# Pool branch's window means as band products, output weights' casts behind the query and key copies, and 20 taps off VectorE, in a two-block transformer kernel

## The chip, the cores and the metric

The kernel runs on one core of a Trainium2 chip. The metric is the device time of one launch in microseconds, from a batch of timed runs; beside it stands one execution taken by the hardware profiler, whose rows are quoted below. In the rows PE is TensorE's matmul, PEld its weight load, DVE is VectorE, ACT ScalarE, POOL GpSimd and SP SyncE, whose queue issues all DMA transfers here. Times in rows are in us from the start of the span unless marked ns.

## The reference

Two different transformer blocks run one after the other on 256 tokens of width 1024, in float32. The first has a stick-breaking attention and a latent attention side by side, a gated feed-forward with a short convolution, and a gate by a second input. The second block, in which the change lies, is:

```
h   = rmsnorm(x) * (1 + scale) + shift                    # scale, shift from c @ mod_w
z   = h @ w_in                                            # split into the inputs of three branches
y_conv = silu(layernorm(conv31(a_val * sigmoid(a_gate)))) # depthwise, 31 taps, 256 channels
y_att  = attention over the 64 keys that an index score picks, 8 heads
y_pool = per group g of 64 channels, window w = 2, 4, 8, 16:
         mean of the last min(t + 1, w) tokens of u, minus u, then @ pool_w[g]; times pool_scale
x  += g1 * (concat(y_conv, y_att, y_pool) @ w_out)
x  += g2 * moe(rmsnorm(x) ...)                            # 32 experts, 2 of them per token
out = rmsnorm(x)
```

The pool branch takes 256 channels of `z`, four groups with one window each.

## The kernel before

Matrix products of the two blocks are made to float32's precision from two parts: a weight or an activation is split into a rounded part (a ScalarE cast) and the rest (a VectorE subtraction, both in `split`), and `mm3` adds three products. Tokens lie in two blocks of 128. A tensor that is contracted over channels lies transposed, channels on partitions, as `hZ` does for the second block's input; projections whose result is wanted with channels on partitions go through `ch_unit` (weights stationary, 256 tokens moving), those with tokens on partitions through `tok_unit` (a token block stationary, up to 256 weight columns moving).

Only TensorE's instructions stand in an order written by hand. For the second block's mixing part that order is the string `ORDER`: each word calls one step. `up` is the pool branch's projection, `qk0` to `qk3` the queries and keys of two heads each, `va` the values, `d0 d1` the scores of the two token blocks, `sm0 sm1` their softmax, `po` the pool branch's last product, `dT` and `do` the transposes and the product with the values, `w0` to `w3` the output weights' load and split, `c60` and so on the product of chunk 6 of the mixed channels for token block 0 with its output weights, `tp` the convolution's taps, `ct co` its transposes and what follows them, and `ea eh el e1 to e4 es` take a buffer into the ring of expert weights and issue its load. The other engines' instructions, SyncE's loads among them, are put in order by the framework's planner, which works with costs of its own and the program's order; each engine then runs its list in order.

What the change touches:

- `up_proj` (L1317): 48 products into one PSUM bank, one copy `pu` to SBUF, channels on partitions and tokens along the row behind 16 zeros. On GpSimd follow sums of shifted copies (`s_a`, `s_b`: windows 2, 4, 8 and 16 by doubling, each on the partitions that need it), a product with 1 / min(t + 1, w) for the first 16 tokens (`rcp`, made at the kernel's start with `winv`), one with 1 / w for the others, and the subtraction of `pu`.
- `pool_out` (L1344): eight products with `pool_w`; ScalarE and VectorE then write chunks 6 and 7 of `mix2`, the two-part input of the output projection.
- `conv_taps` (L1290): the convolution as 31 taps on two channel halves. Half 0 runs wholly on VectorE. Of half 1 the last `N_TAP` taps are ScalarE multiplies into one of six buffers `pr`, which GpSimd adds up in `cb`:

```
act(pr, src[:, 1], AF.Copy, scale=tap[1])
G.tensor_tensor(cb, cb, pr, op=ALU.add)
```

- `qk2` (L1367): three products into one bank, then two ScalarE copies into `q2` and `k2T`; the scores read these.
- `out_weights` (L1400): loads two chunks of output weights into one of three raw buffers and splits them. These buffers are given one after the other to expert weights as well.
- `w2k2` (L1199): tiles of 2 x 256 + 32 columns in five buffers, used by the index scores' relus (`ixr`, eight tiles), `sg`, `pu`, `s_a`, `s_b` and later ones.

The expert stage streams 192 pieces of 1 MB through a ring of 23 buffers, which come free one by one as the mixing part ends: an `es` tile after `dT1`, raw buffers after their splits, the two `mix2` tiles when the last product of the output projection has read them.

Of the kernel before, what the change touches and what calls it, by code (L numbers as in the profile page):

```python
# [10 lines left out]
F32 = mybir.dt.float32  # L11
# [4 lines left out]
ALU = mybir.AluOpType  # L16
# [19 lines left out]
N_A = 5  # L36
N_B = 3
N_C = 3
N_TAP = 12
NORM_ACT = {'d0': 1, 'd1': 1}  # L40
N_POOL = 0
N_2K = 5
# [4 lines left out]
MOE_K = 2  # L47
X_AT = {(2, 9): 4, (31, 9): 1, (31, 10): 1}
LAST = 'y01 y12 x2 m02 y24 m24'
ORDER = 'qi0 kT0 qi1 kT1 ix0 ix1 cv0 li0 li1 cv1 ea ea lo0 lo1 ae lw ea ea ea va0 up eh el qk0 qk1 qk2 qk3 va1 d0 sm0 d1 po sm1 w3 e1 e2 c60 c61 w1 dT0 do0 c70 c71 c20 w2 dT1 c30 do1 tp e3 e4 e4 rl g1 c21 c31 c40 w0 ct e1 e1 c50 c51 c41 es es co'  # L50
W_AT = (2,)
MIX_ENG = 'VV VV'
SET_LATE = (0, 0)
# [14 lines left out]
def block_pair_kernel(ctx, tc, A, out, dbg=None):  # L68
# [63 lines left out]
    def bank(name):  # L132
        return psp.tile([P, 512], F32, tag="b", name=name)
# [58 lines left out]


    PW = 16
    winv = cp.tile([P, 2], F32, name="winv")
    for i, wdt in enumerate((2, 4, 8, 16)):
        G.memset(winv[64 * (i % 2):64 * (i % 2) + 64, i // 2:i // 2 + 1], 1.0 / wdt)
    rcp = cp.tile([P, 2, PW], F32, name="rcp")
    G.iota(rcp[:, 0, :], pattern=[[1, PW]], base=1, channel_multiplier=0, allow_small_or_imprecise_dtypes=True)
    V.reciprocal(rcp[:, 0, :], rcp[:, 0, :])  # L200
    V.tensor_scalar(rcp[:, 1, :], rcp[:, 0, :], winv[:, 1:2], None, op0=ALU.max)
    V.tensor_scalar(rcp[:, 0, :], rcp[:, 0, :], winv[:, 0:1], None, op0=ALU.max)
# [996 lines left out]
    def w2k2(name):  # L1199
        return wk.tile([P, 2 * SEQ + 32], F32, tag="w2kb", name=name, bufs=N_2K)  # L1200
# [108 lines left out]
        G.tensor_tensor(ca[:, 1, :], ca[:, 1, :], cb, op=ALU.add)  # L1309


    TS = slice(PW, PW + SEQ)
    pw = wk.tile([P, 2, 64], F32, name="pw")
    load(pw, A["pool_w"])
    pooled = []

    def up_proj():  # L1317
        upb = bank("pup")
        raw = raw_pk("w_in2_c", 4, (2, KC, P), "r_up")
        for j in range(2):  # L1320
            ch_unit(raw[:, j], upb[:, j * SEQ:(j + 1) * SEQ], hZ, f"w_up2{j}")
        pu, s_a, s_b = [w2k2(nm).rearrange("p (c t) -> p c t", c=2) for nm in ("pu", "s_a", "s_b")]
        for t_ in (pu, s_a, s_b):
            G.memset(t_[:, :, 0:PW], 0.0)
        S.copy(pu[:, :, PW:], upb.rearrange("p (c t) -> p c t", c=2))

        def sh(t, c, rs, k):
            return t[rs, c, PW - k:PW + SEQ - k]

        full, top = slice(0, P), slice(64, P)  # L1330
        G.tensor_tensor(s_a[:, :, TS], pu[:, :, TS], pu[:, :, PW - 1:PW + SEQ - 1], op=ALU.add)
        G.tensor_tensor(s_b[:, 1, TS], sh(s_a, 1, full, 0), sh(s_a, 1, full, 2), op=ALU.add)
        G.tensor_tensor(s_b[top, 0, TS], sh(s_a, 0, top, 0), sh(s_a, 0, top, 2), op=ALU.add)
        G.tensor_copy(s_a[top, 0, TS], s_b[top, 0, TS])
        G.tensor_tensor(s_a[:, 1, TS], sh(s_b, 1, full, 0), sh(s_b, 1, full, 4), op=ALU.add)
        G.tensor_tensor(s_b[top, 1, TS], sh(s_a, 1, top, 0), sh(s_a, 1, top, 8), op=ALU.add)
        G.tensor_copy(s_a[top, 1, TS], s_b[top, 1, TS])
        G.tensor_tensor(s_a[:, :, PW:2 * PW], s_a[:, :, PW:2 * PW], rcp, op=ALU.mult)
        for c in range(2):
            G.tensor_scalar(s_a[:, c, 2 * PW:], s_a[:, c, 2 * PW:], winv[:, c:c + 1], None, op0=ALU.mult)  # L1340
        G.tensor_tensor(s_a[:, :, TS], s_a[:, :, TS], pu[:, :, TS], op=ALU.subtract)
        pooled.append(s_a)

    def pool_out():  # L1344
        pb = [bank(f"ppl{i}") for i in range(2)]
        for c in range(2):
            for par in range(2):
                rs = slice(64 * par, 64 * par + 64)
                T.matmul(pb[par][rs, c * SEQ:(c + 1) * SEQ], pw[rs, c, :], pooled[0][rs, c, TS], start=(c == 0),
                         stop=True, skip_group_check=True)  # L1350
        for c in range(2):
            for par in range(2):
                rs = slice(64 * par, 64 * par + 64)
                src, g_ = pb[par][rs, c * SEQ:(c + 1) * SEQ], cv("pool_scale_2", c, rs)
                hi, lo = [t[rs, 6 + c, :] for t in mix2]
                act(hi, src, AF.Copy, scale=g_)
                V.scalar_tensor_tensor(lo, src, g_, hi.bitcast(F32), op0=ALU.mult, op1=ALU.subtract)
# [5 lines left out]
    def lat_load():  # L1363
        wu = raw_pk("w_lat2", 0, (4, 512), "r_wu")
        lw.extend(wu[:, 2 * i:2 * i + 2] for i in range(2))

    def qk2(c):  # L1367
        o = bank(f"pq2{c}")
        for k in range(2):
            T.matmul(o[:, :SEQ], lw[0][:, k, c * P:(c + 1) * P], lnT[:, k, :], start=(k == 0), stop=(k == 1))  # L1370
        T.matmul(o[:, SEQ:], lw[1][:, 0, c * P:(c + 1) * P], lnT[:, 2, :], start=True, stop=True)
        S.copy(q2[0][:, c, :], o[:, :SEQ])
        S.copy(k2T[:, c, :], o[:, SEQ:])

    def val2(b):
        o = bank(f"pv2{b}")
# [23 lines left out]
    def out_weights(u):  # L1400
        raw = raw_rows("w_out_2", u, f"r_out{u}")
        for j in range(2):
            wpo[2 * u + j] = split(raw[:, j, :], f"w_out{2 * u + j}", (D,), eng=G if 2 * u + j in OUT_G else V)

    def out_chunk(c, b):
        if not acc:
# [42 lines left out]
    def router_load():  # L1449
# [3 lines left out]
        load(M2["rb"], rows_of(A["router_b"], 36))  # L1453

    M2 = {}
    steps = {"lw": lat_load, "up": up_proj, "po": pool_out, "tp": conv_taps, "ct": conv_T,
             "co": conv_out, "rl": router_load, "ea": lambda: grow(ewa, 1),
             "eh": lambda: grow(ap_, 1, "ah", (P, KC, SEQ)), "el": lambda: grow(ap_, 1, "al", (P, KC, SEQ)),
             "ae": lambda: act_set("exp_and_others", SET_LATE[1]),
# [387 lines left out]
def lay_out(inputs):  # L1847
# [35 lines left out]
    o["fcols"] = cw.reshape(4, 44, P).transpose(2, 0, 1)  # L1883
    o["mod_w"] = I["mod_w_2"][0].reshape(KC, P, 3, 2048).transpose(2, 0, 1, 3).reshape(3 * KC, P, 2048)
    w = I["w_in_2"][0]
    o["w_in2_c"] = ch(w, *((a, a + P) for a in (0, 256, 896, 1152, 1480)))
    o["w_in2_q"] = tok(w, [(512, 256)])
    o["w_in2_k"] = tok(w, [(768, 128), (1408, 72)])
    o["pool_w"] = I["pool_w_2"][0].reshape(2, P, 64).transpose(1, 0, 2)
# [31 lines left out]
```

## Time and profile before

| | us |
|---|---|
| median of 3 runs (lowest to highest) | 942.63 (941.95 to 943.38) |
| profiled execution | 942.79 |
| its span, first to last instruction | 941.1 |

| engine | busy us | share of the span |
|---|---|---|
| TensorE matmul | 785.0 | 83% |
| TensorE weight load | 570.9 | 61% |
| VectorE | 466.7 | 50% |
| ScalarE | 321.8 | 34% |
| GpSimd | 110.1 | 12% |

The span falls into the first block (to some 366 us), the second block's mixing part (to some 490 us) and the experts. The shares are averages over these stages. A timeline row gives start, duration, engine, line, operation, output and inputs, a form, and in brackets how long the engine had been idle and what ended that; rows of one line that follow each other are merged, with their count. Many rows of ScalarE have line 80, a helper's, and are told apart by their tiles.

### The profile page before, as it was taken

To read this page: it belongs to the slowest core of one execution; us is meant where nothing else is said; L and a number is where in the kernel's file an instruction comes from. 1 tells how busy PE (TensorE), PEld (TensorE's weight loads), DVE (VectorE), ACT (ScalarE), POOL (GpSimd) and SP (SyncE) were. 2 spreads that over 40 slices of the span, in tenths; PEclk is the share of its full clock that TensorE was granted. 3 is DMA by queue.
4 is the path that set the end of the run, shared out by engine and by line. 5 is a ranking of instruction groups with operands and counts; after the bars stand their busy time and mean duration, and the time that the engine had idled before them with its cause. 6 is when DMAs were issued, how large, how long until landed. Compare 5 with 4: busy or idle time off the path is not lost. (4 is left out here: it accounts for less than half of the span.)

```text
span 941.1 us, 17238 instructions
## 1 busy us (share of the span) xinstructions
PE 785.0 (83%) x7172; PEld 570.9 (61%) x7172; DVE 466.7 (50%) x1011; ACT 321.8 (34%) x636; POOL 110.1 (12%) x176
## 2 busy tenths in 40 slices
PE   6999989999999998996988988677766767766864
PEld 6898859999999775894675645243333433433422
DVE  5777476678888788589963323112121121211113
ACT  5649645555555575465741101000010000100100
POOL 1321320222112112207010000000000000000000
PEclk9999999999999998997999999879799897988887
DMA  8862388588676755745389999999999999999994
GB/s 309 283 206 85 122 333 318 194 338 313 254 276 231 268 203 194 301 168 179 129 332 422 422 420 425 419 425 421 423 422 422 425 422 422 423 421 426 420 423 166
DMA packets 45894, 301.22 MB, mean 320 GB/s; under 512 B 5360, under 2 KB 6388, under 8 KB 11124
## 3 DMA queue, kind: packets, MB, share of 16 engines
q1 hardware_dynamic: 45812, 300.08, 79.9%
q8 instruction: 58, 0.95, 0.4%
q14 instruction: 24, 0.20, 0.1%
HBM read 299.01 MB, written 1.05 MB: 319 GB/s over the span
## 5 line engine op out<-in xcount | busy, mean ns | idle before, releaser
L1710 PE MATMUL eu<-ew,XT 128*32 128x256 f32 x2048 | 141.8, 409 | 51.6 <-DMA ew<-in_exp_dram 51.5
L1710 PEld LDWEIGHTS eu<-ew,XT 128*32 128x32 f32 x2048 | 60.9, 115 | 123.9 <-DMA ew<-in_exp_dram 57.0
L80 ACT ACTIVATE hm<-eu 128x128 f32<-128x128 f32 x32 | 8.9, 278 | 334.2 <-PE eu L1710 334.2
L1737 PE MATMUL ey<-ew,hmT 128*32 128x256 f32 (+2 forms) x1088 | 80.7, 432 | 37.1 <-DMA ew<-in_exp_dram 25.2
L1723 DVE TENSOR_TENSOR hm<-hm,eu 128x128 f32<-128x128 f32 x32 | 9.2, 288 | 145.4 <-ACT hm L80 145.4
L1737 PEld LDWEIGHTS ey<-ew,hmT 128*32 128x32 f32 x1088 | 33.1, 121 | 71.6 <-DMA ew<-in_exp_dram 34.8
L1748 DVE TENSOR_TENSOR eys<-ey,g2y 128x256 f32<-128x256 f32 x31 | 13.2, 425 | 107.5 <-PE ey L1737 107.5
L1008 POOL TENSOR_TENSOR ac<-cv_g,cv_v 128x256 f32<-128x256 f32 x22 | 36.0, 1637 | 154.3 <-ACT w_g_w L80 108.3
L222 POOL TENSOR_SCALAR ep_fin<-msf 128x2 f32<-128x2 f32 x1 | 0.2, 238 | 446.2 <-DVE msf L1827 446.2
L275 PE MATMUL u<-hF_h,w_g_w 128*128 128x256 f32 x168 | 47.6, 283 | 0.0
L273 PE MATMUL u<-hF_h,w_g_w 128*128 128x256 f32 x168 | 47.5, 283 | 0.0
L274 PE MATMUL u<-hF_l,w_g_w 128*128 128x256 f32 x168 | 47.5, 283 | 0.0
L274 PE MATMUL u<-hF_l,w_v_w 128*128 128x256 f32 x160 | 45.3, 283 | 0.0
L275 PE MATMUL u<-hF_h,w_v_w 128*128 128x256 f32 x160 | 45.3, 283 | 0.0
L273 PE MATMUL u<-hF_h,w_v_w 128*128 128x256 f32 x160 | 45.2, 283 | 0.0
L1639 PE MATMUL moe<-eys,gT 32*128 32x256 f32 (+1 forms) x528 | 43.4, 444 | 1.4 <-DVE eys L1761 1.4
L1720 DVE COPY gT<-pgs 128x256 f32<-128x256 f32 x32 | 13.6, 425 | 52.4 <-PE pgs L1706 52.3
L80 ACT ACTIVATE XT<-px,c_SH,c_G 128x128 f32<-128x128 f32 x32 | 14.7, 458 | 63.9 <-DVE XT L1681 63.9
L1673 PEld LDWEIGHTS px<-hr,x 128*128 128x128 f32 x256 | 33.0, 212 | 4.3 <-issue 3.3
L1673 PE MATMUL px<-hr,x 128*128 128x128 f32 x256 | 34.7, 299 | 0.7 <-DVE hr L1665 0.7
L274 PE MATMUL dn<-w_dn_w,ach 128*128 128x512 f32 x88 | 34.6, 393 | 0.0
L1639 PEld LDWEIGHTS moe<-eys,gT 32*128 32x128 f32 x528 | 28.8, 216 | 9.5 <-issue 7.0
(566 smaller groups left out, 1978.1 us busy)
## 6 DMA issues: line engine op xcount, KB each, us to landing
ew<-in_exp_dram SPq DMA_DIRECT2D x189, 1024.0 KB, 19.7
r_mod<-in_mod_w_dram SPq DMA_DIRECT2D x24, 1024.0 KB, 8.7
r_gv<-in_w_up_dram SPq DMA_DIRECT2D x22, 1024.0 KB, 6.3
r_d<-in_w_down_dram SPq DMA_DIRECT2D x11, 1024.0 KB, 5.0
r_wo<-in_w_o_dram SPq DMA_DIRECT2D x4, 1024.0 KB, 4.8
r_pg<-in_w_ple_gate_dram SPq DMA_DIRECT2D x4, 1024.0 KB, 6.1
r_out<-in_w_out_dram SPq DMA_DIRECT2D x4, 1024.0 KB, 4.8
r_v<-in_w_in_t_dram SPq DMA_DIRECT2D x2, 1024.0 KB, 7.2
```

Source lines behind the costliest of these rows:

```text
L80: i = getattr(nc.scalar, name)(*a, **kw)
L273: T.matmul(o, l[0], r[0], start=start, stop=False, skip_group_check=True)
L274: T.matmul(o, l[0], r[1], start=False, stop=False, skip_group_check=True)
L275: T.matmul(o, l[1], r[0], start=False, stop=stop, skip_group_check=True)
L1008: G.tensor_tensor(a_, gt, vl, op=ALU.mult)
L1639: T.matmul(moe[c][:, b * 256:b * 256 + 256][:, js], gT[rs, TB[b]], yt[rs, js], start=(start and b == 0), stop=stop, skip_group_check=True)
L1673: T.matmul(pt[:, j * P:(j + 1) * P], x[b][:, k * P:(k + 1) * P], hr[:, b], start=(b == 0), stop=(b == 1))
L1710: T.matmul(u[32 * g_:32 * g_ + 32, 0:2 * P], XT[:, k, 32 * i:32 * i + 32], etiles[6 * e + k // 2][k % 2][:, :, P * g_:P * g_ + P], start=( ...
L1720: V.tensor_copy(gT, pg[:, :SEQ])
L1723: V.tensor_mul(hm, hm, u[:, P:2 * P])
L1737: T.matmul(y[32 * c:32 * c + 32, 0:64 * (js.stop - js.start)], hmT[:, 32 * k:32 * k + 32], w2e[k].rearrange("p j (c i) -> p c j i", c=4)[: ...
L1748: V.tensor_mul(yt, y[:, 0:256], g2y)
```

## The change

The pool branch's projection now gives tokens on partitions (`puT`), from weights laid out for that (`w_in2_u`). The windows' means minus the input are a product over tokens with a matrix that is 1 / w on a band, less the identity: `band` for all tokens beyond the first 16, `edge` with the shorter counts for these. Both are built in the second block by selects on GpSimd. A new step `pb` makes the 12 products between `qk1` and `qk2`, and `po` moves from behind `d1` to behind `sm0`. `puT` and `pooled` are taken from the `w2kb` buffers before the first step. The casts of output weights get an order edge behind the last query and key copy. `N_TAP` goes from 12 to 20.

```diff
-N_TAP = 12
+N_TAP = 20
-ORDER = '... up eh el qk0 qk1 qk2 qk3 va1 d0 sm0 d1 po sm1 w3 e1 e2 c60 c61 ...'
+ORDER = '... up eh el qk0 qk1 pb qk2 qk3 va1 d0 sm0 po d1 sm1 w3 e1 e2 c60 c61 ...'
-    (winv and rcp at the kernel's start: four memsets, an iota, three VectorE operations)
+    WIN = (2, 4, 8, 16)
+    band, edge = wk.tile([P, 4, P + 16], F32, name="band"), wk.tile([P, 4, 16], F32, name="edge")
+    rt = wk.tile([P, 16], F32, name="rt")
+    G.iota(rt, pattern=[[1, 16]], base=1, channel_multiplier=0, allow_small_or_imprecise_dtypes=True)
+    V.reciprocal(rt, rt)
+    for i, wdt in enumerate(WIN):
+        G.memset(band[:, i], 1.0 / wdt)
+        V.tensor_scalar(edge[:, i], rt, 1.0 / wdt, None, op0=ALU.max)
+    for t_, n in ((band, P + 16), (edge, 16)):
+        G.affine_select(t_, t_, pattern=[[0, 4], [1, n]], compare_op=ALU.is_ge, fill=0.0, base=0, channel_multiplier=-1)
+        for i, wdt in enumerate(WIN):
+            if wdt < n:
+                G.affine_select(t_[:, i], t_[:, i], pattern=[[-1, n]], compare_op=ALU.is_ge, fill=0.0, base=wdt - 1,
+                                channel_multiplier=1)
+        m = min(n, P)
+        V.tensor_sub(t_[:, :, :m], t_[:, :, :m], ident[:, None, :m].to_broadcast([P, 4, m]))
+    puT, pooled = [w2k2(nm)[:, :2 * SEQ].rearrange("p (c t) -> p c t", c=2) for nm in ("puT", "pooled")]
 
     def up_proj():
-        upb = bank("pup")
-        raw = raw_pk("w_in2_c", 4, (2, KC, P), "r_up")
-        for j in range(2):
-            ch_unit(raw[:, j], upb[:, j * SEQ:(j + 1) * SEQ], hZ, f"w_up2{j}")
-        (pu, s_a, s_b: three memsets, the copy pu, eleven GpSimd operations)
+        raw = raw_pk("w_in2_u", 0, (KC, 256), "r_up")
+        o = [bank(f"pup{b}") for b in range(NB)]
+        tok_unit(raw, 256, [t[:, :256] for t in o], hZ, "w_up2")
+        for b in range(NB):
+            S.copy(puT[:, b], o[b][:, :256])
+
+    def pool_band():
+        pb = bank("pband")
         for c in range(2):
+            o = pb[:, c * SEQ:(c + 1) * SEQ]
+            for b, cs_, t_, j in ((0, slice(0, 16), edge, 0), (0, slice(16, P + 16), band, 16), (1, slice(P, SEQ), band, 0)):
+                for par in range(2):
+                    rs = slice(64 * par, 64 * par + 64)
+                    T.matmul(o[rs, cs_], puT[:, b, 128 * c + 64 * par:][:, :64],
+                             t_[:, 2 * c + par, j:j + cs_.stop - cs_.start], start=(c == b == 0 and t_ is edge),
+                             stop=True, skip_group_check=True)
+        S.copy(pooled, pb.rearrange("p (c t) -> p c t", c=2))
@@ qk2
-        S.copy(q2[0][:, c, :], o[:, :SEQ])
-        S.copy(k2T[:, c, :], o[:, SEQ:])
+        qk_ins[:] = [S.copy(q2[0][:, c, :], o[:, :SEQ]), S.copy(k2T[:, c, :], o[:, SEQ:])]
@@ out_weights
-            wpo[2 * u + j] = split(raw[:, j, :], f"w_out{2 * u + j}", (D,), eng=G if 2 * u + j in OUT_G else V)
+            wpo[2 * u + j] = split(raw[:, j, :], f"w_out{2 * u + j}", (D,), eng=G if 2 * u + j in OUT_G else V,
+                                   first=[list(qk_ins)])
```

`split` puts the ScalarE cast behind the instructions in the first list of `first` by an edge of order alone, without a semaphore; the VectorE subtraction gets none, since `first` has one list.

## Rows read from the trace of the kernel before

**Rows 1.** The page's slices of 23.5 us: mean share of the DMA engines.
```profile
DMA  8862388588676755745389999999999999999994
```

**Rows 2.** Windows: length; busy of PE, PEld, DVE, ACT, POOL; granted clock; DMA share; GB/s.
```profile
442.70:451.00 8.30, 7.11 (x21) 4.33 (x22) 7.81 (x29) 6.10 (x22) 0.00 (x0) 0.55 0.16 67
460.00:464.00 4.00, 3.88 (x31) 3.03 (x33) 3.93 (x7) 3.58 (x5) 0.69 (x1) 1.00 0.26 59
465.20:484.30 19.10, 19.10 (x101) 15.39 (x101) 13.38 (x27) 9.19 (x17) 2.00 (x5) 1.00 0.88 345
480.00:488.00 8.00, 7.76 (x51) 6.68 (x50) 6.64 (x18) 4.64 (x13) 1.96 (x4) 1.00 0.57 210
600.00:700.00 100.00, 71.89 (x845) 37.07 (x837) 20.00 (x66) 5.61 (x15) 0.00 (x0) 0.86 1.01 423
```

**Rows 3.** Timeline of SyncE, the issues of two expert pieces.
```profile
461.76 0.33 SPq L142 DMA_DIRECT2D ew<-in_exp_dram  x1
484.34 0.33 SPq L142 DMA_DIRECT2D ew<-in_exp_dram  x1
```

**Rows 4.** Waits: who for whom, us in total, times, longest; 429.5 to 484.5.
```profile
PE ppl L1349 <- POOL s_a L1341: 4.1, 1, 4.1
PE sc_d L775 <- ACT qk L80: 3.1, 2, 2.2
SPq L142 <- PE mo L275: 3.5, 1, 3.5
```

**Rows 5.** Timeline of TensorE's products.
```profile
434.36 4.21 PE L775 MATMUL sc_d<-qk 64*128 64x128 f32 x20 [0.88 <-ACT qk L80]
442.71 1.97 PE L1349 MATMUL ppl<-s_a,pw 64*64 64x256 f32 x8 [4.14 <-POOL s_a L1341]
450.92 1.04 PE L827 MATMUL ppt_d<-ident,es 128*128 128x128 f32 x8
459.00 2.65 PE L827 MATMUL ppt_d<-ident,es 128*128 128x128 f32 x16
462.97 2.28 PE L841 MATMUL o_d<-es,lv 128*64 128x128 f32 x32
470.65 0.60 PE L1420 MATMUL pcl<-ident,ca 128*128 128x128 f32 x4
484.14 0.40 PE L275 MATMUL mo<-w_out_w,mix_l 128*128 128x512 f32 x1
```

**Rows 6.** Timeline of VectorE.
```profile
441.06 4.65 DVE L1298 SCALAR_TENSOR_TENSOR ca<-upad,cols,ca 128x256 f32<-128x256 f32 x9
450.19 0.42 DVE L803 CUSTOM_DVE_ANT_0 es<-sc_d,ixb 128x256 f32<-128x256 f32 x1
451.55 0.69 DVE L832 COPY es<-ppt_d 128x512 f32<-128x512 f32 x1 [0.93 <-PE ppt_d L827]
466.75 2.04 DVE L1298 SCALAR_TENSOR_TENSOR ca<-upad,cols,ca 128x256 f32<-128x256 f32 x4
```

**Rows 7.** Groups by line: count, busy us, mean ns, idle before; the last: whole run.
```profile
L1298 DVE SCALAR_TENSOR_TENSOR ca<-upad,cols,ca 128x256 f32<-128x256 f32 x48 | 24.8, 549 | 0.3
L80 ACT ACTIVATE pr<-upad,cols 128x256 f32<-128x256 f32 x11 | 4.7, 497 | 1.0 <-POOL cb L1308 1.0
L1308 POOL TENSOR_TENSOR cb<-cb,pr 128x256 f32<-128x256 f32 x11 | 9.5, 866 | 3.1 <-ACT pr L80 2.3
L594 POOL TENSOR_SCALAR_AFFINE_SELECT sbt<-sbt 128x256 f32<-128x256 f32 x16 | 6.7, 429 | 34.7 <-DVE sbt L607 22.8 <-ACT sbt L80 11.3 <-DVE nm_m L806 0.6
```

**Rows 8.** Timeline of ScalarE.
```profile
426.35 0.51 ACT L80 ACTIVATE pr<-upad,cols 128x256 f32<-128x256 f32 x1 [0.61 <-POOL cb L1308]
430.67 1.04 ACT L80 CAST w_out_w<-r_out 128x1024 fp32r<-128x1024 f32 x1 [2.40 <-DMA r_out<-in_w_out_dram]
452.67 0.51 ACT L80 ACTIVATE es<-es,nm_d 128x256 f32<-128x256 f32 x1
```

**Rows 9.** Timeline of GpSimd.
```profile
415.50 0.12 POOL L1324 MEMSET pu<- 128x32 f32 x1 [22.09 <-DVE ixa L1262]
```

More of the change, by code (lines that the diff above doesn't have):

```diff
@@ L49 @@
 LAST = 'y01 y12 x2 m02 y24 m24'
-ORDER = 'qi0 kT0 qi1 kT1 ix0 ix1 cv0 li0 li1 cv1 ea ea lo0 lo1 ae lw ea ea ea va0 up eh el qk0 qk1 qk2 qk3 va1 d0 sm0 d1 po sm1 w3 e1 e2 c60 c61 w1 dT0 do0 c70 c71 c20 w2 dT1 c30 do1 tp e3 e4 e4 rl g1 c21 c31 c40 w0 ct e1 e1 c50 c51 c41 es es co'
+ORDER = 'qi0 kT0 qi1 kT1 ix0 ix1 cv0 li0 li1 cv1 ea ea lo0 lo1 ae lw ea ea ea va0 up eh el qk0 qk1 pb qk2 qk3 va1 d0 sm0 po d1 sm1 w3 e1 e2 c60 c61 w1 dT0 do0 c70 c71 c20 w2 dT1 c30 do1 tp e3 e4 e4 rl g1 c21 c31 c40 w0 ct e1 e1 c50 c51 c41 es es co'
 W_AT = (2,)
@@ L194, in block_pair_kernel @@
     PW = 16
[L195 to L202, printed above, removed]
     slots = cp.tile([P, CAP], F32, name="slots")
@@ L1309, in conv_taps @@
         G.tensor_tensor(ca[:, 1, :], ca[:, 1, :], cb, op=ALU.add)
-    TS = slice(PW, PW + SEQ)
     pw = wk.tile([P, 2, 64], F32, name="pw")
     load(pw, A["pool_w"])
-    pooled = []
-    def up_proj():
-        upb = bank("pup")
-        raw = raw_pk("w_in2_c", 4, (2, KC, P), "r_up")
-        for j in range(2):
-            ch_unit(raw[:, j], upb[:, j * SEQ:(j + 1) * SEQ], hZ, f"w_up2{j}")
[L1322 to L1338, printed above, removed]
-        for c in range(2):
-            G.tensor_scalar(s_a[:, c, 2 * PW:], s_a[:, c, 2 * PW:], winv[:, c:c + 1], None, op0=ALU.mult)
-        G.tensor_tensor(s_a[:, :, TS], s_a[:, :, TS], pu[:, :, TS], op=ALU.subtract)
-        pooled.append(s_a)
@@ L1348, in pool_out @@
                 rs = slice(64 * par, 64 * par + 64)
-                T.matmul(pb[par][rs, c * SEQ:(c + 1) * SEQ], pw[rs, c, :], pooled[0][rs, c, TS], start=(c == 0),
+                T.matmul(pb[par][rs, c * SEQ:(c + 1) * SEQ], pw[rs, c, :], pooled[rs, c, :], start=(c == 0),
                          stop=True, skip_group_check=True)
@@ L1365, in lat_load @@
         lw.extend(wu[:, 2 * i:2 * i + 2] for i in range(2))
+    qk_ins = []
     def qk2(c):
@@ L1455, in block_pair_kernel @@
     M2 = {}
-    steps = {"lw": lat_load, "up": up_proj, "po": pool_out, "tp": conv_taps, "ct": conv_T,
+    steps = {"lw": lat_load, "up": up_proj, "pb": pool_band, "po": pool_out, "tp": conv_taps, "ct": conv_T,
              "co": conv_out, "rl": router_load, "ea": lambda: grow(ewa, 1),
@@ L1885, in lay_out @@
     w = I["w_in_2"][0]
-    o["w_in2_c"] = ch(w, *((a, a + P) for a in (0, 256, 896, 1152, 1480)))
+    o["w_in2_c"] = ch(w, *((a, a + P) for a in (0, 256, 896, 1152)))
+    o["w_in2_u"] = tok(w, [(1480, 256)])
     o["w_in2_q"] = tok(w, [(512, 256)])
```

## The prediction

> **What bounds the kernel now.** I began with the slices of the page. The DMA row is ragged in the first half and stands at 9 from slice 22 on [rows 1]: the expert stage is one unbroken stream of weights. The table of windows gives its pace, 423 GB/s at a share of 1.01 [rows 2], so a piece of 1024 KB costs 1048.6 / 423 = 2.48 us. Time can only be won where the engines of DMA idle: 460 to 464 has a share of 0.26 (3.0 us idle) and 480 to 488 one of 0.57 (3.4 us idle) [rows 2]. Next comes what ends that idling. The list of DMA issues shows the first late piece at 461.76 and the one that starts the unbroken stream at 484.34 [rows 3]; the waits say that the latter stood 3.5 us for a product into `mo` [rows 4], and the last of these starts at 484.14 [rows 5]. This piece takes over a `mix2` tile, which is free when the output projection has read it. From there to the end everything hangs on the stream. So the kernel's time moves one for one with the end of the output projection, as long as the pieces before it (from 461.76 on) move too.
>
> What sets 484.1? From 465.2 to 484.3 TensorE has 19.10 busy of 19.10 us at full clock [rows 2]: fixed work. It begins when the second block's attention output (`do1`, 462.97 + 2.28) is done [rows 5]. Followed back: `do1` waits for the transposes `dT1` at 459.00 [rows 5], these for the second softmax, whose exponentials start at 452.67 on ScalarE [rows 8]. They need `nm_d`, which on VectorE stands behind the copy `es<-ppt_d` at 451.55; that copy waited 0.93 us for TensorE's `dT0` at 450.92 [rows 5, 6]. `dT0` stands in TensorE's written order behind `po` and `c60 c61`, and `po` at 442.71 had waited 4.14 us for GpSimd's `s_a` [rows 4, 5]. That is the pool branch's chain of shifted sums, and it is on the path. Close beside it lies VectorE: the last bias-and-maximum of the second softmax ends at 450.19 + 0.42 = 450.61, with nine taps in one row (441.06, 4.65 us) ahead [rows 6].
>
> **The change part by part.**
> *Pool branch.* Off GpSimd go the shifted sums; the last of them ended as `po` began. In their place: the same 48 products of the projection (token-major instead of channel-major: equal in number and columns), two copies of 256 columns instead of one of 512, 12 small products, one copy of 512 columns. A small product costs about 2.28 / 32 = 71 ns by `do1` [rows 5], so 0.9 us, or 1.7 at half clock. TensorE then stood 3.1 us before scores that wait for the query and key copies [rows 4]; these cover it, and without cover it costs 0.9 to 1.7. `po` goes ahead of `d1` and finds its input ready: the 4.14 us wait goes.
> What is late next is `nm_d`. Without the coupling through `dT0` the exponentials start when the bias-and-maximum ends: 452.67 - 450.61 = 2.1, less the `nm_d` instruction itself (some 0.2): 1.9 us. That is the low end for this chain.
> *The band matrices* take 4 memsets, 9 selects and an iota on GpSimd and seven instructions on VectorE. A select of 256 columns took 429 ns [rows 7]; the one over 4 x 144 columns is then about 1.0 us, the others at most 0.43: an estimate of 5 us in all. GpSimd was idle for 22.09 us before 415.50 [rows 9], so they cost nothing there, unless one lands ahead of a small norm operation: 0 to 1 us, I take 0.
> *Buffers.* `puT` and `pooled` hold two of five `w2kb` buffers while the index scores run, so three are left for eight `ixr` tiles and `sg`. In the trace a buffer of the second token block's `ixr` came free only at 415.50, after VectorE's top-8 rounds [rows 9]. One relu, and then `sg`, now waits for that; ScalarE runs in order, so the `lv` copies behind `sg` may slip by 0 to 2 us. The same 3.1 us of cover takes it: 0.
> *Output weights' casts.* One cast stood in ScalarE's queue between the query and key copies and waited 2.40 us for its DMA [rows 8]; that and the casts made the scores wait 3.1 us [rows 4]. With the order the copies go first, which brings the scores forward by 0 to 3.1. It pays only if VectorE can take them earlier, so it is in the VectorE term. The other side: the raw buffer is freed later, so the next `r_out` load goes out later; its weights aren't multiplied before `c20`, after `dT0`. I take 0 and keep the bad case as a rival.
> *20 taps.* VectorE loses 8 instructions of 549 ns [rows 7], 4.4 us. ScalarE gets 8 x 497 ns = 4.0 us, GpSimd 8 x 866 ns = 6.9 us [rows 7], where the pool sums used to be. VectorE has 7.81 busy of 8.30 us in 442.7 to 451 [rows 2]: work taken from it there shifts what follows. How much lies ahead of 450.61 is the planner's choice: none (0) to all (4.4). I take half, 2.2, since taps stand on both sides of it. The page "GPSIMD Engine Reference" of the Trainium skill (8. Key points) speaks against this part: GpSimd shares SBUF interfaces with VectorE and contends with its two-input operations. The nine taps of [rows 6], mostly beside an idle GpSimd, take 517 ns each against the mean of 549; by the rule, the taps left could lose some 0.4 us and the sum would be -3.7.
>
> **Sum.** 1.9 + 2.2 = 4.1 us off the chain to `do1`; bounds 1.9 and 6.3. A second limit: `ct` at 470.65 needs all taps, which end at 466.75 + 2.04 = 468.79 [rows 5, 6]: slack 1.9, and 4.4 from the fewer taps, together 6.3. So up to 6.3 the fixed 19.1 us simply move forward. The profiled execution took 942.79 us (span 941.1 and 1.7 around it); 942.79 - 4.1 = 938.7. The median of the runs is 0.16 lower: I forecast 938.5.
>
> **The rivals.**
> *More: all eight taps and a waking clock, -6.3, 936.3 us.* In 442.7 to 451 TensorE was granted 0.55, about the 1.2 GHz level, right after its waits in front of the scores and of `po` [rows 2, 4]. If those waits go, `c60 c61` run at 2.4 GHz, stop delaying `dT0`, and VectorE sets the path with all 4.4 us gone. "TensorE: Matmul & The Clock Gate" in the Trainium skill (What's actually happening) says that the low clock is the default and that sustained activity releases it; that agrees with these rows, and by it the full gain needs TensorE to be fed. Against: the scores still wait for VectorE's reads of their banks. 0.20.
> *Less: VectorE fills the gap with other taps, only the coupling goes, less 0.7 for band products that aren't covered: -1.2, 941.4 us.* For: GpSimd's wait was only 4.1 of about 8 us of stalls. 0.18, with another 0.04 for a stream whose earlier pieces don't move.
> *Slower: ScalarE's queue.* A tap's multiply already waited 0.61 us for GpSimd's sum to give back a buffer, just ahead of the query and key copies [rows 8]. With 19 of them the queue runs at GpSimd's pace; if the eight new ones stand ahead of the copies, these lose 8 x 0.866 = 6.9 us, less 2.4 of DMA wait and 2.1 of casts that are gone from there: scores 2.4 us later. The two casts (2.1) then fall between copies and exponentials: 4.5 later, less the 1.9: +2.6, 945.2 us. It decides from the point where the last key copy ends later than the 434.4 at which the scores went on [rows 5]. Against: I take it that the planner puts a ready copy ahead of a tap, which stands later in the program. 0.13.
>
> **How the numbers follow.** Forecast 0.45, more 0.20, less 0.22, slower 0.13. Under 0.2% (1.9 us) this kernel's measurement can't tell a change from none. Faster takes the forecast, the "more" case and a fifth of "less": 0.69; same the rest of "less": 0.18; slower 0.13. The range reaches a little past "more" (935.3) and into the slower case (943.6).
>
> **What would show it.** `ppl` no longer waits for GpSimd and stands before the second scores; the exponentials of the second softmax start at about 448.5 instead of 452.67; `do1` ends near 461 and the last `mo` product near 480.4; the stream from there is as dense as before. It is wrong if the exponentials don't move, if ScalarE shows waits of `pr` on `cb` ahead of the `qk` copies, or if the share of DMA is low before the piece that takes the `mix2` tile.

## The result and the profile after

The changed kernel is slower: 947.52 us (median of 4, 946.52 to 948.32) against 942.29 us (4 runs of the kernel before on the same chip, 941.81 to 943.38); ratio 1.0056, 95% interval 1.0041 to 1.0071, some 5 us. Forecast were 938.5 us, with a range of 935.3 to 943.6. The profiled execution took 947.66 us, span 946.0. The ratios leave out five executions of 965 to 1841 us, each well above the others of its kernel.

The rows begin with SyncE: the issue of the first output weights' load (a mark that stands ahead of all that the change moves; 404.05 before), of the first late expert piece, and of the piece that takes the `mix2` tile [rows 3]. The second fence is the TensorE rows that answer to [rows 5].
```profile
405.39 0.33 SPq L142 DMA_DIRECT2D r_out<-in_w_out_dram  x1
...
466.63 0.33 SPq L142 DMA_DIRECT2D ew<-in_exp_dram  x1
...
488.44 0.33 SPq L142 DMA_DIRECT2D ew<-in_exp_dram  x1
```
```profile
435.96 1.04 PE L767 MATMUL sc_d<-qk 64*128 64x128 f32 x8 [2.73 <-ACT qk L80]
436.93 1.08 PE L1348 MATMUL ppl<-pooled,pw 64*64 64x256 f32 x8
437.94 0.70 PE L767 MATMUL sc_d<-qk 64*128 64x256 f32 x4
443.92 3.35 PE L767 MATMUL sc_d<-qk 64*128 64x256 f32 x12 [5.28 <-DVE mx_d L795]
...
456.36 1.97 PE L833 MATMUL o_d<-es,lv 128*64 128x128 f32 x16 [2.94 <-DVE es L824]
...
464.32 1.91 PE L819 MATMUL ppt_d<-ident,es 128*128 128x128 f32 x16
...
467.55 2.02 PE L833 MATMUL o_d<-es,lv 128*64 128x128 f32 x32
...
488.25 0.39 PE L267 MATMUL mo<-w_out_w,mix_l 128*128 128x512 f32 x1
```
The piece goes out 4.1 us later than in [rows 3], right behind a last `mo` product that is 4.1 us later too; the stream behind it is as dense as before (below, 600 to 700). The pool projection no longer waits for GpSimd, as forecast. In its place the second scores wait 5.28 us for VectorE: they take PSUM banks that the first softmax must read first. VectorE, ScalarE's exponentials of the second softmax and GpSimd show why:
```profile
435.04 0.81 DVE L1263 TENSOR_SCALAR ixb<-ixa 128x256 f32<-128x256 f32 x1
435.77 6.54 DVE L1290 SCALAR_TENSOR_TENSOR ca<-upad,cols,ca 128x256 f32<-128x256 f32 x9
442.23 1.21 DVE L283 TENSOR_TENSOR w_out_w<-r_out,w_out_w 128x1024 fp32r<-128x1024 f32 x1
443.37 0.28 DVE L795 CUSTOM_DVE_ANT_0 es<-sc_d,ixb 128x128 f32<-128x128 f32 x1
```
```profile
455.42 0.51 ACT L80 ACTIVATE es<-es,nm_d 128x256 f32<-128x256 f32 x1
```
```profile
423.43 16.55 POOL L1300 TENSOR_TENSOR cb<-cb,pr 128x256 f32<-128x256 f32 x19 [27.28 <-ACT pr L80]
```
The selection mask `ixb` is ready at 435.85 and the first scores at 437.0, yet VectorE's queue has nine taps and a subtraction of output weights before the first bias-and-maximum at 443.37. And these taps are slow: 6.54 / 9 = 0.73 us each, a mean over two kinds: by their starts the first five, up to 440.18, take 0.86 to 0.94 us each beside the additions, the next two 0.40 when the additions are over. Windows of TensorE (length, busy, ..., granted clock third from the end) show the wait, what follows it, and the stream:
```profile
438.64:443.92 5.28, 0.00 (x2) 0.00 (x1) 5.24 (x12) 1.00 (x3) 2.09 (x3) 0.79 0.00 0
443.92:448.00 4.08, 4.08 (x14) 2.98 (x15) 3.98 (x18) 2.44 (x12) 0.00 (x0) 0.50 0.01 2
600.00:700.00 100.00, 71.89 (x830) 36.27 (x833) 19.44 (x64) 5.40 (x15) 0.00 (x0) 0.85 1.01 422
```

**A caution for all comparisons.** The code before 366 us is the same in all kernels here, up to the few operations on `winv` and `rcp` at the start that the changed ones don't have, but their traces differ there: the first output weights' load goes out between 402.33 and 408.49. TensorE's clock explains part of it. One stretch of the first block, for the kernel after and for the seventh of the experiments below:
```profile
94.00:97.00 3.00, 3.00 (x18) 0.61 (x12) 2.51 (x6) 1.93 (x2) 0.12 (x1) 0.50 0.02 5
```
```profile
94.00:97.00 3.00, 3.00 (x27) 2.54 (x28) 2.23 (x4) 2.52 (x6) 1.46 (x2) 1.00 0.36 52
```
With TensorE busy all the 3 us, the clock was granted at half in the one and fully in the other: the same 16 products into `mod` take 3.40 us in the one and 1.92 in the other, and the distance between the two traces grows from 1.2 us ahead of this stretch to 2.9 behind it. The 1.2 us were there from the first 12 us of the program on; their cause is open. So positions of single traces are given here from the mark on, and times by the ratios. Of the 4.9 us between the two profiled spans, 1.3 arose before the mark, 2.8 between the mark and the last `mo` product, 0.8 in the stream.

The table has, for each kernel, the ratio to the kernel before (same chip, 95% interval) and positions in us from the mark (from each kernel's rows by subtraction): end of the last key copy, first bias-and-maximum of the first softmax, exponentials of the second, transposes `dT1`, end of `do1`, last `mo` product.

| kernel | ratio | copies | max 1 | exp 2 | `dT1` | `do1` | `mo` |
|---|---|---|---|---|---|---|---|
| before | 1 | 30.2 | 34.4 | 48.6 | 54.9 | 61.2 | 80.1 |
| after | 1.0056 (1.0041 to 1.0071) | 31.1 | 38.0 | 50.0 | 58.9 | 64.2 | 82.9 |
| 1 after_no_edge | 0.9997 (0.9987 to 1.0006) | 31.3 | 35.1 | 45.6 | 52.4 | 58.8 | 77.5 |
| 2 after_tap12 | 1.0020 (1.0011 to 1.0029) | 26.9 | 34.7 | 45.8 | 55.2 | 60.4 | 79.1 |
| 3 after_band_only | 0.9964 (0.9951 to 0.9977) | 30.9 | 34.0 | 44.4 | 50.8 | 56.7 | 76.3 |
| 4 before_edge_only | 1.0015 (1.0002 to 1.0028) | 25.7 | 35.8 | 50.6 | 56.9 | 62.9 | 81.7 |
| 5 before_tap20_only | 1.0046 (1.0032 to 1.0060) | 29.5 | 34.4 | 51.7 | 58.2 | 65.0 | 83.7 |
| 6 after_po_back | 1.0084 (1.0070 to 1.0099) | 31.1 | 38.0 | 51.5 | 62.6 | 67.8 | 86.5 |
| 7 after_taps_behind | 1.0000 (0.9991 to 1.0009) | 31.1 | 33.7 | 45.8 | 53.1 | 59.5 | 78.3 |
| 8 after_tap12_behind | 1.0023 (1.0012 to 1.0035) | 26.9 | 30.8 | 42.8 | 51.6 | 56.9 | 80.4 |
| 9 after_thin_adds | 1.0006 (0.9984 to 1.0028) | 28.3 | 33.5 | 45.6 | 53.2 | 58.4 | 77.1 |
| 10 after_ten_buffers | 1.0035 (1.0021 to 1.0049) | 28.3 | 38.0 | 50.0 | 58.7 | 63.9 | 82.6 |
| 11 after_tap16_behind | 0.9968 (0.9954 to 0.9982) | 28.6 | 31.5 | 43.5 | 51.9 | 57.1 | 76.7 |
| 12 band_only_tap4 | 1.0025 (1.0010 to 1.0041) | 30.8 | 33.1 | 43.5 | 49.9 | 55.8 | 80.5 |
| 13 taps_and_subs_behind | 0.9983 (0.9965 to 1.0000) | 31.1 | 33.7 | 44.8 | 51.4 | 58.1 | 77.1 |
| 14 tap18_and_subs_behind | 0.9972 (0.9956 to 0.9988) | 29.4 | 31.5 | 43.3 | 49.6 | 56.5 | 76.0 |

### The profile page after: what moved, and what is told of

Same layout as the page of the kernel before. It is cut to its first block, busy times and chain, and to the rows that moved or that the text cites. A ratio compares the mean times of both kernels' runs of the same rounds, so it can differ in the third digit from the quotient of the medians.

```text
span 946.0 us, 17298 instructions
## 1 busy us (share of the span) xinstructions
PE 786.3 (83%) x7196; PEld 568.8 (60%) x7196; DVE 465.4 (49%) x1007; ACT 325.5 (34%) x646; POOL 108.1 (11%) x179
## 5 line engine op out<-in xcount | busy, mean ns | idle before, releaser
L1711 PE MATMUL eu<-ew,XT 128*32 128x256 f32 x2048 | 141.7, 406 | 60.6 <-DMA ew<-in_exp_dram 60.4
L1738 PE MATMUL ey<-ew,hmT 128*32 128x256 f32 (+2 forms) x1088 | 84.7, 450 | 30.1 <-DMA ew<-in_exp_dram 18.1
L1640 PE MATMUL moe<-eys,gT 32*128 32x256 f32 (+1 forms) x528 | 40.2, 416 | 1.3 <-DVE eys L1762 1.3
L80 ACT ACTIVATE XT<-px,c_SH,c_G 128x128 f32<-128x128 f32 x32 | 14.6, 457 | 62.9 <-DVE XT L1682 62.9
L266 PE MATMUL dn<-w_dn_w,ach 128*128 128x512 f32 x88 | 34.6, 393 | 0.0
L265 PE MATMUL dn<-w_dn_w,ach 128*128 128x512 f32 x88 | 34.6, 393 | 0.0
L267 PE MATMUL dn<-w_dn_w,acl 128*128 128x512 f32 x88 | 34.6, 393 | 0.0
```

Source lines behind the costliest of these rows:

```text
L80: i = getattr(nc.scalar, name)(*a, **kw)
L265: T.matmul(o, l[0], r[0], start=start, stop=False, skip_group_check=True)
L266: T.matmul(o, l[0], r[1], start=False, stop=False, skip_group_check=True)
L267: T.matmul(o, l[1], r[0], start=False, stop=stop, skip_group_check=True)
L1640: T.matmul(moe[c][:, b * 256:b * 256 + 256][:, js], gT[rs, TB[b]], yt[rs, js], start=(start and b == 0), stop=stop, skip_group_check=True)
L1711: T.matmul(u[32 * g_:32 * g_ + 32, 0:2 * P], XT[:, k, 32 * i:32 * i + 32], etiles[6 * e + k // 2][k % 2][:, :, P * g_:P * g_ + P], start=( ...
```

## The experiments

**1 to 4: which part costs?** Each part undone or done alone. Three theories stood against each other: E blames the order, by way of VectorE's list, Q ScalarE's queue behind 20 taps, and B the PSUM banks of the band products and the earlier pool projection. "The order" is the one that puts the output weights' casts behind the last query and key copies.
```diff
 # 1 after_no_edge (2 and 3: see N_TAP; 4 adds the same order to the kernel before)
-            wpo[2 * u + j] = split(..., first=[list(qk_ins)])
+            wpo[2 * u + j] = split(...)
 # 2 after_tap12; 3 after_band_only has this and the edit of 1
-N_TAP = 20
+N_TAP = 12
```


> The changed kernel without the order between the key copies and the output weights' casts; band products and 20 taps stay. Theory E (the order is the cause: with the subtractions of the output weights gone from the top-8 rounds, VectorE's list has nine taps and one subtraction ahead of the first softmax): here the first bias-and-maximum follows at once on the second selection mask; exponentials of the second softmax at 449 to 451 us, time 938 to 942. Theory Q (20 taps clog ScalarE at GpSimd's pace): still 945 to 948, key copies end at 436 or later. Theory B (the band products, the earlier pool projection and the turn of PSUM banks): still 945 to 948, with the second scores waiting for VectorE's reads of the first ones' banks.

> The changed kernel with 12 taps on ScalarE and GpSimd again; band products and the order stay. Theory E: taps and a subtraction still ahead of the first softmax, 946 to 949. Theory Q: no multiply waits ahead of the key copies, 937 to 941. Theory B: 945 to 948.

> The changed kernel with 12 taps and without the order: only the band products and the earlier pool projection are left of the change. Theory E: 939 to 942, the gain of the pool branch by itself. Theory Q: 938 to 941. Theory B: 945 to 948; so this run tells B from both others.

> The kernel before with only the order between the key copies and the output weights' casts added; shifted sums on GpSimd and 12 taps as before. Theory E: seven taps and a subtraction stand ahead of the first softmax, 945 to 948. Theories Q and B: 941 to 943, no change.

No theory was right alone. Against the kernel before (942.6 us, so 0.1% is 0.94 us): the band products alone -3.4 us; 20 taps on top of them +3.1 (0.9997 against 0.9964); the order on top of them +5.3 (1.0020 against 0.9964). The sum, +5.0, is the change as measured (+5.3): on this base the parts add, and two of them cost. On the kernel before they don't: there the order costs only 1.4 us (0.2 to 2.6, run 4) and 20 taps 4.3 (run 5 below), so most of what the order costs comes with the band products. Theory B falls with run 3. The order (E) and the 20 taps each cost; whether the taps cost by ScalarE's queue (Q) is taken up below.

With the order alone (4), both blocks' scores are done by 432.84 without a wait (two SyncE marks differ by 0.06 us, so [rows 5] compare directly: 438.57 there). What the order was to give, it gives, 5.7 us of it; nobody takes it up:
```profile
429.64 3.20 PE L775 MATMUL sc_d<-qk 64*128 64x128 f32 x32
442.08 1.97 PE L1349 MATMUL ppl<-s_a,pw 64*64 64x256 f32 x8 [9.23 <-POOL s_a L1341]
```
```profile
434.62 4.23 DVE L1298 SCALAR_TENSOR_TENSOR ca<-upad,cols,ca 128x256 f32<-128x256 f32 x7
...
439.92 0.28 DVE L803 CUSTOM_DVE_ANT_0 es<-sc_d,ixb 128x128 f32<-128x128 f32 x1
```
VectorE's queue was fixed beforehand by the planner's list, which has seven taps and a subtraction before the first softmax, though all scores have been there since 432.84 and the mask since 434.70. In run 2 it is ten taps, and a second place shows (VectorE, then TensorE):
```profile
434.18 4.04 DVE L1290 SCALAR_TENSOR_TENSOR ca<-upad,cols,ca 128x256 f32<-128x256 f32 x10
438.14 1.21 DVE L283 TENSOR_TENSOR w_out_w<-r_out,w_out_w 128x1024 fp32r<-128x1024 f32 x1
...
448.96 1.22 DVE L283 TENSOR_TENSOR w_out_w<-r_out,w_out_w 128x1024 fp32r<-128x1024 f32 x1
...
450.17 1.22 DVE L283 TENSOR_TENSOR w_out_w<-r_out,w_out_w 128x1024 fp32r<-128x1024 f32 x1
451.31 0.69 DVE L824 COPY es<-ppt_d 128x512 f32<-128x512 f32 x1
```
```profile
452.05 1.98 PE L833 MATMUL o_d<-es,lv 128*64 128x128 f32 x16 [3.68 <-DVE es L824]
```
The subtractions that the order pushed back stand ahead of the copy of the first transposes, and the first attention output waits 3.68 us for it. This second place is what the kernel before is spared: from the second exponentials to `dT1` the order takes the distance from 6.4 to 9.4 us with the band products (runs 3 and 2), and leaves it at 6.3 without (before and run 4).

**5 and 6: the taps alone, and the banks.**
```diff
 # 5 before_tap20_only (the kernel before)
-N_TAP = 12
+N_TAP = 20
 # 6 after_po_back
-ORDER = '... d0 sm0 po d1 sm1 ...'
+ORDER = '... d0 sm0 d1 po sm1 ...'
```


> The kernel before with only 20 taps instead of 12 on ScalarE and GpSimd. Theory C (the taps cost by contention: VectorE's taps beside GpSimd's additions took 0.73 us each in the changed kernel, 0.40 beside an idle GpSimd with 12 taps): VectorE loses 2 to 3 us ahead of the second softmax and GpSimd's shifted sums come later, 944 to 947. Theory Q (ScalarE's queue): the key copies end 2 us or more later and set the scores, 944 to 947 also, but with the score products waiting for copies that end behind 437. If the taps are harmless without the order of the casts: 941 to 943.

> The changed kernel with the pool projection back behind the second scores, as it stood before, so that the second scores take other PSUM banks. Theory B (the turn of the banks makes the second scores wait for VectorE's reads of the first): the second scores end before 440 and the time falls by 2 us or more, 943 to 945.5. Theory E: the second softmax comes behind the first on VectorE anyway, 946 to 948.5.

Run 6 goes against theory B: with other banks the second scores don't wait for VectorE, but the projection then waits 3.06 us for the same reads, and the kernel is the slowest of all. Run 5 shows best what the taps suffer. The nine taps of [rows 6] stand in the same place, with GpSimd's additions now beside them (VectorE, then GpSimd, then VectorE's taps of the whole run as count, busy, mean ns):
```profile
441.25 7.93 DVE L1298 SCALAR_TENSOR_TENSOR ca<-upad,cols,ca 128x256 f32<-128x256 f32 x9
```
```profile
441.37 0.93 POOL L1308 TENSOR_TENSOR cb<-cb,pr 128x256 f32<-128x256 f32 x1
442.26 1.44 POOL L1341 TENSOR_TENSOR s_a<-s_a,pu 128x512 f32<-128x512 f32 x1
443.67 6.09 POOL L1308 TENSOR_TENSOR cb<-cb,pr 128x256 f32<-128x256 f32 x7
```
```profile
L1298 DVE SCALAR_TENSOR_TENSOR ca<-upad,cols,ca 128x256 f32<-128x256 f32 x40 | 24.7, 630 | 0.5
```
4.65 us have become 7.93, 0.88 each: nine taps beside nine instructions of GpSimd, one for one. (Of the nine in [rows 6], eight took 0.40 each and one 1.40, behind GpSimd's last sum of 1.35 us.) Over the whole run 40 taps take 24.7 us where 48 took 24.8 [rows 7]. Eight taps were taken off VectorE and it got nothing for them. The page "SBUF — State Buffer" of the Trainium skill (Who interferes with whom) says that a VectorE instruction with two SBUF inputs and a GpSimd instruction that reads SBUF exclude each other, and that the one that comes second waits for the other's end; one tap per addition agrees with that.

Two things limit this reading. Where a tap alternates with an instruction of the top-8 rounds, the same additions lengthen it far less. In the changed kernel, with GpSimd's additions running from 423.43 to 439.98, such taps take 0.54 and 0.47 us from start to next start:
```profile
430.15 0.61 DVE L1290 SCALAR_TENSOR_TENSOR ca<-upad,cols,ca 128x256 f32<-128x256 f32 x1
430.69 0.08 DVE L1261 MATCH_VALUE_LOAD ixa<-m,ixa 128x8 f32 x1
...
431.09 0.55 DVE L1290 SCALAR_TENSOR_TENSOR ca<-upad,cols,ca 128x256 f32<-128x256 f32 x1
431.56 0.42 DVE L1260 MAX8 m<-ixa 128x8 f32<-128x256 f32 x1
```
And taps slow down without any additions. Seven taps with GpSimd idle, in run 2 and in run 5:
```profile
451.91 2.85 DVE L1290 SCALAR_TENSOR_TENSOR ca<-upad,cols,ca 128x256 f32<-128x256 f32 x7
```
```profile
456.61 3.60 DVE L1298 SCALAR_TENSOR_TENSOR ca<-upad,cols,ca 128x256 f32<-128x256 f32 x7
```
In run 2 (12 taps on ScalarE and GpSimd) the two halves still alternate here, 0.41 us each; in run 5 (20 taps there) half 1 has no taps left on VectorE, and those of half 0 follow each other, 0.51 us each. All 16 traces show this step: beside an idle GpSimd 0.39 to 0.40 us from one tap's start to the next's up to the last tap of half 1, and 0.50 to 0.52 behind it. That each tap of half 0 then adds to what the one just before it wrote is the likely reason; no run tests it. With eight more taps in this state VectorE loses 8 x 0.12 = 1.0 us besides the contention.

Nor does run 5 tell the ways to the time apart. ScalarE's multiplies there wait for GpSimd's sums ahead of the first softmax's exponentials, which start 3.6 us later from the mark than before, and by way of `mix_h` this reaches `c60`, ahead of `dT0` (before, then run 5's ScalarE and TensorE):
```profile
441.28 0.40 ACT L80 ACTIVATE es<-es,nm_d 128x128 f32<-128x128 f32 x1 [6.49 <-DVE nm_d L806]
```
```profile
440.36 0.51 ACT L80 ACTIVATE pr<-upad,cols 128x256 f32<-128x256 f32 x1 [4.97 <-POOL cb L1308]
...
444.61 0.51 ACT L80 ACTIVATE pr<-upad,cols 128x256 f32<-128x256 f32 x1 [1.76 <-POOL cb L1308]
445.02 0.38 ACT L80 ACTIVATE es<-es,nm_d 128x128 f32<-128x128 f32 x1
```
```profile
449.10 0.80 PE L273 MATMUL mo<-w_out_w,mix_h 128*128 128x512 f32 x1 [3.37 <-ACT mix_h L80]
```
In run 5 ScalarE's queue is thus a second way beside VectorE's taps (3.3 us), at another place than theory Q said: the key copies end 0.7 us sooner (29.5 against 30.2), not 2 later.

**7 and 8: VectorE's order by itself.** Same order of the casts, but the taps from the 14th on wait in the list for the first softmax.
```diff
 # 7 after_taps_behind; 8 after_tap12_behind has N_TAP = 12 too
-                    V.scalar_tensor_tensor(ca[:, c, :], ...)
+                    s = V.scalar_tensor_tensor(ca[:, c, :], ...)
+                    n_v[0] += 1
+                    if n_v[0] > 13:
+                        tc.add_manual_dep(s.ins, bm['d0'].ins.name, NOSYNC, reason='order')
```


> The changed kernel with one thing more: the nine taps that stood in VectorE's queue between the second selection mask and the first softmax are ordered behind its last bias-and-maximum; the order of the casts, the band products and the 20 taps stay. Theory E (what the order of the casts costs is only that the list fills the time it frees with taps, ahead of scores that are already there): the first bias-and-maximum starts at 437 to 439 instead of 443.4, the second scores lose most of their 5.3 us wait, the exponentials of the second softmax start at 449 to 451 instead of 455.4, time 941 to 944. If instead the later casts, subtractions and loads themselves cost the time: 946 to 948.

> The changed kernel with 12 taps and with VectorE's later taps (from the 14th) ordered behind the first softmax's last bias-and-maximum. Theory E: the scores of the first block are ready at 432.8 and the mask at 434.3, so the first bias-and-maximum starts at 435.5 instead of 439.3; 4 us earlier, 939 to 942, unless the displaced taps then make the transposes of the convolution wait (1 to 3 us given back, which shows as a wait of those for the taps). If the order of VectorE were not the cause: 944 to 946 as with 12 taps alone.

Run 7 gives back 5.3 us (1.0000 against 1.0056), with the first bias-and-maximum 4.3 and the exponentials 4.3 us sooner: what stands in VectorE's list ahead of the first softmax is shown to be the place. It isn't order alone, since the taps put back come when GpSimd's additions are over, and take 0.41 us each instead of 0.73:
```profile
440.56 1.66 DVE L1294 SCALAR_TENSOR_TENSOR ca<-upad,cols,ca 128x256 f32<-128x256 f32 x4
```
Order alone shows in run 8 against run 2, where the additions are over in both: the first bias-and-maximum comes some 4 us sooner, the exponentials 3.0. But the forecast of run 8's time missed. It isn't faster than run 2, because now the displaced taps end last:
```profile
467.75 0.66 PE L1428 MATMUL pcl<-ident,ca 128*128 128x128 f32 x4 [2.66 <-DVE ca L1294]
```

**9 to 12: contention or ScalarE's queue, and how many taps.**
```diff
 # 9 after_thin_adds
-                    G.tensor_tensor(cb, cb, pr, op=ALU.add)
+                    G.tensor_tensor(cb[:, :16], cb[:, :16], pr[:, :16], op=ALU.add)
 # 10 after_ten_buffers
-N_PR = 6
+N_PR = 10
 # 11 after_tap16_behind: run 7 with N_TAP = 16; 12 band_only_tap4: run 3 with N_TAP = 4
```


> The changed kernel with GpSimd's additions of the 19 tap products done on 16 of 256 columns only, so the convolution's second half is left incomplete; every engine's order of instructions is that of the changed kernel. Theory C (VectorE's taps are slowed by GpSimd's additions beside them): the nine taps ahead of the first softmax take 3.6 to 4.2 us instead of 6.5, the first softmax comes 3 to 5 us earlier, time 943 to 945. Theory Q (ScalarE's multiplies wait for GpSimd to give back buffers): those waits go too and the key copies end about 2 us earlier, but the nine taps still take 6.5 us; 946 to 947.5.

> The changed kernel with ten buffers instead of six for ScalarE's tap products, so that its multiplies wait less for GpSimd's additions; the additions are as many as before and every engine's order of instructions is the same. Theory Q: the key copies end 1.5 to 2 us earlier and the time falls by 1.5 to 2, 945.5 to 946. Theory C: the key copies end earlier, the nine taps and a subtraction still stand ahead of the first softmax and are still slow, no change, 947 to 948.

> The changed kernel with 16 taps and VectorE's taps from the 14th on ordered behind the first softmax: a mean of two runs already done, meant to keep the order of the casts, have less contention than 20 taps and leave fewer taps to the end than 12. If contention and the late taps are both eased: 939 to 941.5. If either decides still: 942 to 945, with 12 taps' 2.7 us wait of the transposes for the last taps halved.

> The band products alone, with 4 taps instead of 12 on ScalarE and GpSimd and the order of the casts as before. Theory C: VectorE gets eight taps of 0.40 us more, and is rid of eight additions of 0.88 us beside it, each of which lengthened its taps by about 0.4; the two cancel ahead of the second softmax, and only the last taps come later: 940 to 942.5, against 940.3 with 12. If the taps on GpSimd were worth their time on VectorE (0.40 to 0.55 us each): 943 to 945.

In 9 and 10 every engine has the instructions of the changed kernel in the same order. The nine taps ahead of the first softmax in run 9, then in run 10, and run 10's second scores:
```profile
430.70 4.11 DVE L1290 SCALAR_TENSOR_TENSOR ca<-upad,cols,ca 128x256 f32<-128x256 f32 x9
```
```profile
436.55 6.51 DVE L1290 SCALAR_TENSOR_TENSOR ca<-upad,cols,ca 128x256 f32<-128x256 f32 x9
```
```profile
444.67 3.35 PE L767 MATMUL sc_d<-qk 64*128 64x256 f32 x12 [8.03 <-DVE mx_d L795]
```
With the short additions, which are over by then, the taps take 0.46 us, not 0.73, and the kernel is 4.7 us faster (1.0006 against 1.0056); its key copies end 2.8 us sooner too, so run 10 is needed beside it. With ten buffers the key copies end 2.8 us sooner in the trace and the second scores just wait longer, 8.03 us; no position behind changes by over 0.3 us. So by the trace theory Q falls as the path of this kernel. By the times alone it doesn't: the ratio is 0.2% lower, which is the 1.5 to 2 us that theory Q forecast, with overlapping intervals, and the trace gives no reason for it. Run 12 missed its forecast: the second softmax does come sooner with fewer additions (43.5 against 44.4 in run 3), more than the cancelling that theory C forecast, but the last taps cost far more than I had put down for them. The transposes of the convolution, in run 12, run 3 and run 11:
```profile
473.90 0.63 PE L1420 MATMUL pcl<-ident,ca 128*128 128x128 f32 x4 [4.17 <-DVE ca L1290]
```
```profile
468.13 0.63 PE L1420 MATMUL pcl<-ident,ca 128*128 128x128 f32 x4 [0.70 <-DVE ca L1290]
```
```profile
467.82 0.63 PE L1428 MATMUL pcl<-ident,ca 128*128 128x128 f32 x4 [0.68 <-DVE ca L1294]
```
There are two limits: the way to `do1`, which contention lengthens, and the end of VectorE's taps, which GpSimd's share shortens. 16 taps with the right order (11) come near both, and this kernel beats before and after.

**13 and 14: the subtractions.** Left open was why `dT1` starts 7.4 to 11.1 us behind the second exponentials in the kernels that have both the order and the band products, and 6.3 to 6.8 in the others (the order alone, run 4, has 6.3 too).
```diff
 # 13 taps_and_subs_behind, on top of 7; 14 has N_TAP = 18 too
-ORDER = '... c60 c61 w1 dT0 do0 ...'
+ORDER = '... c60 c61 dT0 w1 do0 ...'
...
+                if name in ('w_out2', 'w_out3'):
+                    tc.add_manual_dep(lo.ins, bm['Td0'].ins.name, NOSYNC, reason='order')
```


> The changed kernel with its nine taps behind the first softmax, and besides with the casts and subtractions of output weights' chunks 2 and 3 taken up behind VectorE's copy of the first transposes (in the last but two runs of this kind that copy stood behind two subtractions of 1.2 us). If these subtractions are on the path: the first attention output no longer waits 3.7 us for the copy, the second transposes start 1.5 to 3 us sooner after the second softmax's exponentials (7.3 us before), time 940 to 941.5 against 942.8. If ScalarE's normalisation sets the second transposes anyway: no change, 942 to 943.5.

> The same with 18 taps instead of 20: two additions of GpSimd's fewer beside VectorE, two taps more for VectorE. If the subtractions are on the path and contention is eased: 939 to 941, the fastest yet; if the last taps become the limit again: a wait of the convolution's transposes of 0.5 us or more, 940.5 to 942.

TensorE in run 13, `do0`:
```profile
447.29 1.17 PE L837 MATMUL o_d<-es,lv 128*64 128x128 f32 x16 [1.13 <-DVE es L828]
```
In run 7 this wait was 3.68 us; the distance falls from 7.4 to 6.6 us in 13 and to 6.3 in 14, and the position of the last `mo` from 78.3 to 77.1 and 76.0. The times follow (0.9983, 0.9972), though 0.9983 isn't told apart from 1.0000 by the intervals. Run 14 waits 0.66 us for the last taps again and is no faster than 11 or than the band products alone (0.9964), which are the simplest and which none of the others beats.

## Why the prediction was wrong

- **What bounds the kernel**: right. The piece with the `mix2` tile moved by +4.1 us, the last `mo` by +4.1, and the stream behind runs at 422 against 423 GB/s, with 0.8 us more at the end. "One for one" is too strong for the times: from run to run they follow the last `mo` only within some us (see what stays open).
- **Pool branch, -1.9**: right in mechanism, too small. Alone it gives -3.4 us (interval -4.6 to -2.2); the projection doesn't wait, the exponentials come 4.2 us sooner from the mark (44.4 against 48.6), and `nm_d` no longer waits for the `dT0` copy. Building the band matrices cost what I took, about nothing: from 366 us, ahead of the building, to the mark behind it no kernel that has them loses more than 0.3 us on the kernel before. Their products come behind the mark, and no run tells their cost apart.
- **20 taps, -2.2: the first step that failed.** "VectorE loses 8 instructions of 549 ns, 4.4 us" took a mean that already held the contention, and the contention was put down at 0.4 us, from nine taps of 517 ns "mostly beside an idle GpSimd". An idle GpSimd gives 0.40 (4.04 / 10 in run 2), so eight taps were worth 3.2 us at most. In a row beside its additions a tap takes 0.88, and once half 1 has none left on VectorE 0.51 even without them. Together these take away again what the eight taps save (24.7 against 24.8 us in all), and ahead of the second softmax they take more: +3.1 us on the band products, +4.3 on the kernel before, there also by way of ScalarE.
- **Order of the casts, 0: the second step that failed.** The copies did end sooner (25.7 against 30.2 with the order alone). But "it pays only if VectorE can take them earlier" was left at a sentence, and the other side was looked for in a late weight. What came was another list on VectorE: the time freed by the subtractions was filled with taps ahead of the first softmax, and the subtractions came back ahead of a copy. +5.3 us on the band products, +1.4 on the kernel before, where the subtractions don't come back ahead of that copy. Run 7 gives back as much by putting the taps behind the first softmax, where they also escape the additions.
- **The rivals.** The slower one, ScalarE's queue at GpSimd's pace, has its condition met (the last key copy ends at 436.45, behind 434.4; from the mark it is 0.8 us later than before, not the 2.4 of the forecast), its multiplies wait for `cb` as written, and its time, 945.2, is nearest to the result. It isn't the path in the changed kernel: run 10 takes these waits away and moves nothing behind in its trace. The "less" case named what did happen, that VectorE fills the gap with other taps, but priced it as a smaller gain and not as a loss.
- **Signs**: `ppl` as forecast; the exponentials at 455.42 instead of 448.5, `do1` ends at 469.57 instead of 461. That the exponentials came later instead of sooner pointed to the way ahead of them.

What stays open: the trace of the changed kernel shows 2.8 us between mark and last `mo`, the times 5.3 us. The rest lies in offsets before the mark and in the stream (from the last `mo` to the end 457.0 us before, 457.4 to 460.3 in the others), and one trace for each kernel doesn't tell a cause there from chance. In all runs but the fourth the time lies above what the position of the last `mo` gives, by 0.4 to 3.6 us; since all are compared with the one trace of the kernel before, that can also lie in this trace.

## What to carry to other kernels

Work moved from VectorE to GpSimd can give VectorE nothing where both then run two-input instructions in a row: price an elementwise instruction by its duration beside a silent GpSimd and beside a busy one, look at what it alternates with, and take all of that from rows. Where a planner fixes an engine's order beforehand, an edge on one engine rewrites the queue of another: ask what its list will put into the time that the edge frees, and what the pushed-back work will stand in front of. When three edits come together, run each alone before combining them.

## What the runs showed of the hardware that I had not expected

A 128x256 multiply-add of VectorE with two SBUF inputs, in a row of such, takes 0.40 us beside an idle GpSimd (ten in 4.04, run 2) and 0.88 us beside a stream of GpSimd additions (nine in 7.93, run 5), one for one with them, and the additions go on at 0.87 us each (19 in 16.55, changed kernel). Alternating with top-8 instructions it takes 0.47 to 0.54 beside the same additions. With GpSimd idle, taps on one half alone take 0.51 against 0.41 where two halves alternate (seven in 3.60 and 2.85). The small masks suffer too: the 128x256 `ixb` took 0.28 us in run 2 and 0.81 in the changed kernel. And the same code in the same place ran at half or at full TensorE clock from one trace to the next (0.50 or 1.00 in 94 to 97 us, with TensorE busy all the time), which put everything behind it some 1.6 us later and is part of what the traces differ by ahead of the mark.
